# SSD x blocks turned into token rows without TensorE, and gated scores in float32r parts

## The chip, the core and the metric

The kernel runs on one core of a Trainium2 chip. The metric is device time in microseconds of one execution. Five engines work from their own in-order queues: TensorE (PE in the profile; PEld is its weight load), VectorE (DVE), ScalarE (ACT), GpSimd (POOL) and SyncE (SP), which issues nearly all transfers. They meet through semaphores.

## What is computed

The reference is a two-layer trunk over 16 learned tokens and 256 frames, so 272 rows of width 2048. Layer 0 has four gated linear-attention heads (GLA) and eight stick-breaking heads behind one input and one output projection. Layer 1 is an SSD mixer with eight groups of eight heads. Two pieces matter here, cut from it:

```python
# layer 0, a gated head: q_dec = q*exp(g_cum), k_inv = k*exp(-g_cum)
scores = jnp.einsum('bcthk,bcshk->bchts', q_dec, k_inv)
scores = jnp.where(causal, scores, 0.0)
o_intra = jnp.einsum('bchts,bcshv->bcthv', scores, v)

# layer 1, SSD: x after convolution and SiLU, per group
xdt = x * dt[..., None]
cb = jnp.einsum('bctgn,bcsgn->bctsg', c_c, b_c)
y_diag = jnp.einsum('bctsgh,bcsghp->bctghp', l_mat * cb[..., None], xdt)
y = y_diag + y_off + d_skip * x_c
y = _rms_norm_groups(y * jax.nn.silu(z), norm_w, SSM_GROUPS)
```

Everything is float32. The kernel evaluates the scan in a quadratic form over 128 rows.

## The kernel before, in words

**Weights and units.** The work is a list of units of 128 x 2048 weights (1 MB each). An input unit makes 128 output channels for all tokens: 16 blocks of 128 x 128 weights, and for each block three float32r products that stand for one float32 product (L178, L179, L180: high x high, high x low, low x high). An output unit does the same with L494 to L496. So TensorE sees a base stream of products of 272, 260, 256 or 512 columns, 48 to a unit. A unit's weights are loaded by SP into one of three `raw` tiles (L144), and cut into halves; for each half ScalarE writes the high part `whi` (L159) and VectorE, or for some halves GpSimd, the low part `wlo` (L160). There are five buffers of each.

**What sets the order.** Everything else (gates, scans, norms) is written as generators that are stepped once at every quarter unit, a `yield` being one step. What a step issues is placed by a list scheduler that simulates a timeline when the program is built; the order on each engine is then fixed.

**Layer 1.** A group's units come in this order: B, C, four of x, four of z (the gate), and then the four output units of the group two before. `post_x` (L1174) convolves each x unit on ScalarE and VectorE into `xt`, channels on partitions; after every second x unit `x_path` activates two of them. The scan needs x with tokens on partitions, multiplied by dt, in `xd` (128 rows of two blocks) and `xd2` (the last 16 rows). `x_path` gets there by eight TensorE transposes against an identity (L1206) into PSUM, a ninth for the last 16 rows of all four tiles (L1209), and VectorE multiplications out of PSUM (L1218, L1224). `mix_ssd` then multiplies xd with the decay matrices M (L1267) and the last rows (L1273), about six units after the last x unit.

**Layer 0.** The values of both kinds of heads are already turned into token rows in another way: `v_blocks` transposes blocks of 32 x 32 on VectorE (L588, L589), and `to_tokens` writes the result to DRAM (L602, L603) and reads it back with the blocks in their places (L606, L610). In `mix_gla` a gated head's scores are float32 products: L721 (128 x 272, two halves of the contraction), L723 (128 x 144) and L725 (16 x 16).

Of the kernel before, what the change touches and what calls it, by code (L numbers as in the profile page):

```python
# [6 lines left out]
F32 = mybir.dt.float32  # L7
F32R = mybir.dt.float32r
AF = mybir.ActivationFunctionType
ALU = mybir.AluOpType  # L10
PSUM = bass.MemoryType.PSUM

P = 128
# [6 lines left out]
T = NM + S  # L20
# [10 lines left out]
NG, HPG = 8, 8  # L31
# [51 lines left out]
def _wait(*tasks):  # L83
    for t in tasks:
        while not t.done:
            yield


class _Body:
# [621 lines left out]
    def mix_gla(self, h):  # L711
        nc, lp = self.nc, self.lp
        act, vec, mm = nc.scalar.activation, nc.vector, nc.tensor.matmul
        q, k = self.cur["q", h], self.cur["k", h]
        v = self.cur["v", h]
        g = self.cur["r", h]
        yield from _wait(self.tasks["r", h], *[self.tasks["v", h, j] for j in (1, 3)])

        zb = self.zbank()
        for j in range(2):  # L720
            mm(zb[:, 16:288], k[:, j, 0:128], q[:, j, 0:272], start=j == 0, stop=j == 1)  # L721
        for j in range(2):
            mm(zb[:, 288:432], k[:, j, 128:256], q[:, j, 272:416], start=j == 0, stop=j == 1)  # L723
        for j in range(2):
            mm(zb[:16, 0:16], k[:, j, 256:272], q[:, j, 416:432], start=j == 0, stop=j == 1)  # L725
        yield
        s = self.spad
        act(s, zb[:, :432], AF.Copy)
        self.causal(s[:, 16:144], 128, False)
        self.causal(s[:, 288:416], 128, False)  # L730
        self.causal(s[:16, 0:16], 16, False)
        yield
        st = self.s2[h % 2]
        sp = self.parts_of(s, st, (0, 0, 1))[2]
        yield
        u = lp.tile([P, 4, T], F32, tag="gu", name=self.nm("gu"))
        sq = lp.tile([P, T], F32, tag="gsq", name=self.nm("gsq"))
        for j in range(4):
            o = self.po()
            self.values(o, *v, slice(j * P, (j + 1) * P), sp, st)  # L740
            vec.tensor_tensor(u[:, j, :], o[:, :T], g[:, j, :], op=ALU.mult)
            if j == 0:
                act(sq, o[:, :T], AF.Square)
            else:
                s2 = lp.tile([P, T], F32, tag="gs2", name=self.nm("gs2"), bufs=2)
                act(s2, o[:, :T], AF.Square)
                nc.gpsimd.tensor_tensor(sq, sq, s2, op=ALU.add)
            yield
        yield
        qh, ql, _ = self.parts_of(sq)  # L750
        yield
        ms = self.po()
        mm(ms[:, :T], self.ones_r, qh, start=True, stop=False)
        mm(ms[:, :T], self.ones_r, ql, start=False, stop=True)
        yield
        m = lp.tile([P, T], F32, tag="gs2", name=self.nm("gms"), bufs=2)
        r = lp.tile([P, T], F32, tag="grs", name=self.nm("grs"))
        vec.tensor_scalar(m, ms[:, :T], 1.0 / GDV, RMS_EPS, op0=ALU.mult, op1=ALU.add)
        act(r, m, AF.Ln)
        act(r, r, AF.Exp, scale=-0.5)  # L760
        self.newton(r, m, sq)
        yield
        mh, ml = self.mix_tile(h)
        for j in range(4):
            vec.scalar_tensor_tensor(u[:, j, :], u[:, j, :], self.col(C_GN, 4 * h + j), r, op0=ALU.mult, op1=ALU.mult)
            act(mh[:, j, :], u[:, j, :], AF.Copy)
            vec.tensor_tensor(ml[:, j, :], u[:, j, :], mh[:, j, :].bitcast(F32), op=ALU.subtract)
            yield
# [405 lines left out]
    def post_x(self, ps, g, j):  # L1174
# [6 lines left out]
        if j % 2:  # L1181
            self.tasks["x", g, j] = self.push(self.x_path(g, j - 1))

    def x_path(self, g, j):
        nc, vec = self.nc, self.nc.vector
        xt = self.cur["x", g]
        xd = self.cur["xd", g]
        self.silu1(xt[:, j : j + 2, :].rearrange("p a t -> p (a t)"), vec)
        yield
        yield  # L1190
        yield
        if g == 0:
            yield from _wait(self.tasks["dt"])
        if j == 0:
            return
        nc.scalar.activation(self.xq[:, :, :NM], xt[:, :, 256:T], AF.Copy)
        for _ in range(5):
            yield
        pin = self.tc.keep_in_program_order

        pts = [self.po(), self.po()]
        p2 = self.zbank()
        for pt, jj in zip(pts, (0, 2)):
            for i in range(2):
                for t in range(2):
                    pin(nc.tensor.transpose(  # L1206
                        pt[:, t * 256 + i * P : t * 256 + (i + 1) * P], xt[:, jj + i, t * P : (t + 1) * P], self.ident
                    ))
        pin(nc.tensor.transpose(p2[:, :P], self.xq.rearrange("p b t -> p (b t)"), self.ident))  # L1209
        yield  # L1210
        hv = lambda a: a.rearrange("p (h c) -> p h c", c=64)
        bd = lambda a: a.rearrange("p (h o) -> p h o", o=1)
        for pt, jj in zip(pts, (0, 2)):
            h0 = g * HPG + 2 * jj
            c = slice(jj * P, jj * P + 256)
            for t in range(2):
                d = bd(self.est[:, 1, t, h0 : h0 + 4]).broadcast_to([P, 4, 64])
                vec.tensor_tensor(hv(xd[:, t, c]), hv(pt[:, t * 256 : (t + 1) * 256]), d, op=ALU.mult)  # L1218
            yield
        e2 = bd(self.est2[:, 1, g * HPG : (g + 1) * HPG])  # L1220
        for j in range(2):
            for p in range(2):
                h, r = 4 * p + 2 * j, 32 * (2 * p + j)
                vec.tensor_tensor(  # L1224
                    self.xd2[32 * j : 32 * j + 16, 2 * p : 2 * p + 2, :], hv(p2[r : r + 16, :P]),
                    e2[:, h : h + 2, :].broadcast_to([16, 2, 64]), op=ALU.mult,
                )
        yield
# [273 lines left out]
```

## Time and profile before

| | us |
|---|---|
| median of three runs | 1371.52 (1371.16 to 1372.23) |
| the profiled execution | 1372.14 |
| its span | 1370.4 |
| TensorE busy in the span | 1361.3 |
| VectorE busy | 1034.8 |
| ScalarE busy | 790.8 |
| GpSimd busy | 255.3 |

The page gives totals by engine, the chain of work that ended last, and the costliest groups of instructions. A timeline row has start, duration, engine, line, tiles and a count. On TensorE consecutive matmuls overlap in the records, so that a duration there is longer than the distance from one start to the next; the difference of two starts is what the engine needs. A float32 product stands there as two records, a float32r product as one.

### The profile page before, as it was taken

What the parts mean: (1) busy time and instruction counts of PE and PEld (TensorE: products, weight loads), DVE (VectorE), ACT (ScalarE), POOL (GpSimd) and SP (SyncE); (2) the same over time, 40 slices, a digit from 0 to 9 for tenths busy, and PEclk for the clock granted to TensorE, in tenths of its full rate; (3) what the DMA queues carried; (4) which work ended last, traced back from release to release, by engine and by line L of the source; (5) the groups of instructions that cost most, each with busy time, mean ns of one, the idle gap of its engine ahead of it and who ended that gap; (6) DMA issues with size and microseconds to landing.
All of it is one profiled execution on the core that took longest, in us unless ns stands there. A gap on an engine that the chain in (4) does not pass through costs nothing.

```text
span 1370.4 us, 26152 instructions
## 1 busy us (share of the span) xinstructions
PE 1361.3 (99%) x10563; PEld 1313.8 (96%) x10563; DVE 1034.8 (76%) x1747; ACT 790.8 (58%) x1221; POOL 255.3 (19%) x253
## 2 busy tenths in 40 slices
PE   9999999999999999999999999999999999999998
PEld 8999999999999999999999999899898999989986
DVE  7858586685665675568899888787877879877688
ACT  6646455355345554556587888556565655656551
POOL 0000010010001100004400124231422323233221
PEclk9999999999999999999999999999999999999999
DMA  9655546456445455554355665465645565555561
GB/s 328 212 177 193 176 163 210 154 169 208 175 160 183 150 194 175 192 166 158 128 185 176 242 222 210 160 229 185 220 170 208 179 206 213 185 185 185 187 213 62
DMA packets 61945, 256.73 MB, mean 187 GB/s; under 512 B 26176, under 2 KB 29056, under 8 KB 33408
## 3 DMA queue, kind: packets, MB, share of 16 engines
q1 hardware_dynamic: 61104, 254.27, 53.7%
q8 instruction: 83, 1.36, 0.4%
q10 hardware_dynamic: 720, 0.79, 0.2%
q14 instruction: 38, 0.31, 0.1%
HBM read 249.29 MB, written 5.74 MB: 186 GB/s over the span
## 4 chain that ended last, share of the span: by engine, by line
PE 97%; DVE 1%; DMA 1%; ACT 0%; issue 0%; SPq 0%; ACTq 0%
PE pj L178 26%; PE pj L179 26%; PE pj L180 26%; PE pj L494 4%; PE pj L496 4%; PE pj L495 4%; PE po L1267 2%; PE po L633 1%; PE po L1206 1%; DMA raw<-in_wts 0%; PE z L1155 0%; DVE acc L503 0%; DVE fst L1415 0%; PE z L721 0%; DMA hacc<-in_xT 0%; PE z L820 0%
## 5 line engine op out<-in xcount | busy, mean ns | idle before, releaser
L178 PE MATMUL pj<-xhi,whi 128*128 128x272 f32 (+4 forms) x2560 | 732.0, 286 | 1.8 <-ACT xhi L330 0.7
L179 PE MATMUL pj<-xlo,whi 128*128 128x272 f32 (+4 forms) x2560 | 730.2, 286 | 0.0
L180 PE MATMUL pj<-xhi,wlo 128*128 128x272 f32 (+4 forms) x2560 | 729.9, 286 | 0.0
L159 ACT ACTIVATE whi<-raw 128x1024 fp32r<-128x1024 f32 (+2 forms) x434 | 449.2, 1038 | 369.3 <-PE pj L179 296.3
L160 DVE TENSOR_TENSOR wlo<-raw,whi 128x1024 fp32r<-128x1024 f32 (+2 forms) x405 | 504.8, 1251 | 196.5 <-ACT whi L159 192.2
L178 PEld LDWEIGHTS pj<-xhi,whi 128*128 128x128 f32 x2560 | 482.4, 189 | 4.6 <-ACT whi L159 1.7
L179 PEld LDWEIGHTS pj<-xlo,whi 128*128 128x128 f32 x2560 | 482.0, 188 | 1.4 <-issue 0.8
L180 PEld LDWEIGHTS pj<-xhi,wlo 128*128 128x128 f32 x2560 | 481.9, 188 | 0.4 <-issue 0.4
L179 PE MATMUL pj<-mixl,whi 128*128 128x272 f32 x384 | 111.1, 290 | 0.0
L178 PE MATMUL pj<-mixh,whi 128*128 128x272 f32 x384 | 110.7, 289 | 0.1
L180 PE MATMUL pj<-mixh,wlo 128*128 128x272 f32 x384 | 110.2, 287 | 0.0
L160 POOL TENSOR_TENSOR wlo<-raw,whi 128x1024 fp32r<-128x1024 f32 x29 | 74.1, 2557 | 171.8 <-ACT whi L159 157.0
L494 PE MATMUL pj<-whi,yh 128*128 128x512 f32 (+1 forms) x240 | 93.2, 388 | 0.0
L495 PE MATMUL pj<-wlo,yh 128*128 128x512 f32 (+1 forms) x240 | 92.6, 386 | 0.0
L496 PE MATMUL pj<-whi,yl 128*128 128x512 f32 (+1 forms) x240 | 92.2, 386 | 0.0
L179 PEld LDWEIGHTS pj<-mixl,whi 128*128 128x128 f32 x384 | 72.4, 188 | 0.2
L178 PEld LDWEIGHTS pj<-mixh,whi 128*128 128x128 f32 x384 | 72.1, 188 | 0.4 <-ACT mixh L847 0.3
L180 PEld LDWEIGHTS pj<-mixh,wlo 128*128 128x128 f32 x384 | 72.4, 188 | 0.0
L261 POOL TENSOR_TENSOR gr<-gr,gsc 128x1088 f32<-128x1088 f32 x6 | 15.4, 2568 | 287.4 <-ACT gsc L260 287.4
L503 DVE SCALAR_TENSOR_TENSOR acc<-pj,rr,acc 128x512 f32<-128x512 f32 (+1 forms) x65 | 46.5, 733 | 10.9 <-PE pj L496 10.7
L496 PEld LDWEIGHTS pj<-whi,yl 128*128 128x128 f32 x240 | 45.1, 188 | 9.1
L494 PEld LDWEIGHTS pj<-whi,yh 128*128 128x128 f32 x240 | 45.1, 188 | 8.9
(340 smaller groups left out, 1443.6 us busy)
## 6 DMA issues: line engine op xcount, KB each, us to landing
raw<-in_wts SPq DMA_DIRECT2D x212, 1024.0 KB, 4.9
ebc<-edr SPq DMA_DIRECT2D x8, 1664.0 KB, 6.3
raw<-in_wts SPq DMA_DIRECT2D x9, 256.0 KB, 6.4
vdr<-vt SPq DMA_DIRECT2D x8, 256.0 KB, 4.9
vt<-vdr SPq DMA_DIRECT2D x32, 64.0 KB, 2.5
hacc<-in_xT SPq DMA_DIRECT2D x7, 272.0 KB, 5.4
early<-in_wts SPq DMA_DIRECT2D x2, 512.0 KB, 6.8
vdr<-vt SPq DMA_DIRECT2D x8, 128.0 KB, 3.4
```

Of the source, the lines that this page charges most:

```text
L159: self.nc.scalar.activation(hi, src, AF.Copy)
L160: eng.tensor_tensor(lo, src, hi.bitcast(F32), op=ALU.subtract)
L178: mm(ps, whi, xhi, start=first, stop=False)
L179: mm(ps, whi, xlo, start=False, stop=False)
L180: mm(ps, wlo, xhi, start=False, stop=last)
L261: mul(c, c, e, op=ALU.mult)
L494: mm(ps, yh[:, kk, tt], hi[:, k, :], start=kk == 0, stop=False)
L495: mm(ps, yh[:, kk, tt], lo[:, k, :], start=False, stop=False)
L496: mm(ps, yl[:, kk, tt], hi[:, k, :], start=False, stop=kk == 3)
L503: self.nc.vector.scalar_tensor_tensor(a, ps, r[:, t : t + 1], a, op0=ALU.mult, op1=ALU.add)
L633: mm = lambda r, a, b, start=False, stop=False: self.nc.tensor.matmul(r, a, b, start=start, stop=stop, skip_group_check=True)
L1267: pin(mm(ov[p][i * 64 : (i + 1) * 64, jj, t0:S], xd[:, s, h * 64 : (h + 1) * 64], M[:, h, c0:c1], start=(s, jj) == (0, 0), stop=False, **gk,))
```

## The change

The diff has two parts. In `mix_gla` the decayed q and k are cut into a high part (ScalarE) and a low part (VectorE) for the first token block and for the last 16 tokens, and those scores become three float32r products each; the middle product (128 x 144) stays float32. One more step (a quarter unit) lies between the cut and the products. In `x_path` groups 2 to 7 (the third to the eighth) leave for a new generator `x_blocks`, once for every two x units: VectorE transposes 32 x 32 blocks out of `xt` in SBUF, SP writes them to DRAM and reads them back by token rows into the same tile, and six steps later VectorE multiplies them with dt into xd and xd2. Groups 0 and 1 keep the TensorE transposes.

```diff
+        kp = lp.tile([P, 2, 2, 144], F32R, tag="kp", name=self.nm("kp"))
+        qp = lp.tile([P, 2, 2, 288], F32R, tag="qp", name=self.nm("qp"))
+        for p, a, cuts in ((kp, k, ((0, 0, 128), (128, 256, 16))), (qp, q, ((0, 0, 272), (272, 416, 16)))):
+            for o, c, n in cuts:
+                hi = p[:, 0, :, o : o + n]
+                act(hi, a[:, :, c : c + n], AF.Copy)
+                vec.tensor_tensor(p[:, 1, :, o : o + n], a[:, :, c : c + n], hi.bitcast(F32), op=ALU.subtract)
+        abj = [(a, b, j) for a, b in ((0, 0), (0, 1), (1, 0)) for j in range(2)]
+        yield
         zb = self.zbank()
-        for j in range(2):
-            mm(zb[:, 16:288], k[:, j, 0:128], q[:, j, 0:272], start=j == 0, stop=j == 1)
+        for n, (a, b, j) in enumerate(abj):
+            mm(zb[:, 16:288], kp[:, a, j, 0:128], qp[:, b, j, 0:272], start=n == 0, stop=n == 5)
         for j in range(2):
             mm(zb[:, 288:432], k[:, j, 128:256], q[:, j, 272:416], start=j == 0, stop=j == 1)
-        for j in range(2):
-            mm(zb[:16, 0:16], k[:, j, 256:272], q[:, j, 416:432], start=j == 0, stop=j == 1)
+        for n, (a, b, j) in enumerate(abj):
+            mm(zb[:16, 0:16], kp[:, a, j, 128:144], qp[:, b, j, 272:288], start=n == 0, stop=n == 5)
...
+    def x_blocks(self, g, j):
+        nc, vec, sync = self.nc, self.nc.vector, self.nc.sync
+        xt, xd = self.cur["x", g], self.cur["xd", g]
+        vt = self.lp.tile([P, 640], F32, tag="xvt", name=self.nm("xvt"), bufs=2)
+        blk = vt[:, :512]
+        o = blk.rearrange("q (b c x) -> q b c x", c=2, x=32)
+        for i in range(2):
+            vec.transpose(o[:, :, i, :], xt[:, j + i, :256].rearrange("p (b x) -> p b x", x=32))
+            vec.transpose(vt[:, 512 + 32 * i : 544 + 32 * i], xt[:, j + i, 240:T])
+        d = self.tc.dram_tile([4, 32, 8, 64], F32, name=self.nm("xdr"))
+        d9 = self.tc.dram_tile([4, 32, 64], F32, name=self.nm("xdr9"))
+        sync.dma_start(d.rearrange("p t b x -> (p t) (b x)"), blk)
+        sync.dma_start(d9.rearrange("p t x -> (p t) x"), vt[:, 512:576])
+        v = blk.rearrange("q (s p x) -> q s p x", s=2, p=4)
+        for b in range(4):
+            sync.dma_start(v[32 * b : 32 * b + 32], d[:, :, b::4].rearrange("p t s x -> t s p x"))
+        t2 = [vt[32 * i : 32 * i + 16, 512:640] for i in range(2)]
+        for i in range(2):
+            sync.dma_start(t2[i].rearrange("q (p x) -> q p x", p=4), d9[:, 16:, 32 * i : 32 * i + 32].rearrange("p t x -> t p x"))
+        for _ in range(6):
+            yield
...
         self.silu1(xt[:, j : j + 2, :].rearrange("p a t -> p (a t)"), vec)
         yield
+        if g > 1:
+            yield from self.x_blocks(g, j)
+            return
```

TensorE in group 3, in the third z unit (`pj` is the unit's PSUM tile, `xhi` and `xlo` the parts of the layer's input). Before:

```order
L179 MATMUL pj_11509<-xlo,whi_11450 128x256
L180 MATMUL pj_11509<-xhi,wlo_11451 128x256
L1206 MATMUL po_11526<-ident,xt_11148 128x128 x4
L1206 MATMUL po_11527<-ident,xt_11148 128x128 x4
L1209 MATMUL z_64<-ident,xq 128x128
L178 MATMUL pj_11509<-xhi,whi_11450 128x256
L179 MATMUL pj_11509<-xlo,whi_11450 128x256
```

Of the change, the same place:

```order
L178 MATMUL pj_11642<-xhi,whi_11579 128x256
L179 MATMUL pj_11642<-xlo,whi_11579 128x256
L180 MATMUL pj_11642<-xhi,wlo_11580 128x256
L178 MATMUL pj_11642<-xhi,whi_11579 128x256
L179 MATMUL pj_11642<-xlo,whi_11579 128x256
```

The nine transposes are gone and nothing took their place; in layer 1 all else on TensorE stands where it stood.

VectorE in group 3, from the second pair of x tiles to the first output unit. Before:

```order
L1089 TENSOR_TENSOR xt_11148<-xt_11148,xcl_11398 128x544
L160 TENSOR_TENSOR wlo_11558<-raw_11447,whi_11557 128x1024
L160 TENSOR_TENSOR wlo_11596<-raw_11507,whi_11595 128x1024
L1085 TENSOR_SCALAR xcl_11537<-gz_11445 128x512
L1218 TENSOR_TENSOR xd_11149<-po_11526,est 128x256 x2
L1218 TENSOR_TENSOR xd_11149<-po_11527,est 128x256 x2
L1224 TENSOR_TENSOR xd_8248<-z_64,est_8840 16x128 x4
L160 TENSOR_TENSOR wlo_11624<-raw_11507,whi_11623 128x1024
L160 TENSOR_TENSOR wlo_11657<-raw_11592,whi_11656 128x1024
L160 TENSOR_TENSOR wlo_11704<-raw_11652,whi_11703 128x1024
```

Of the change (`xvt` is the tile of blocks, `est` holds dt):

```order
L1098 TENSOR_TENSOR xt_11242<-xt_11242,xcl_11513 128x544
L1201 STREAM_TRANSPOSE xvt_11531<-xt_11242 128x8x32
L1202 STREAM_TRANSPOSE xvt_11531<-xt_11242 128x32
...
L160 TENSOR_TENSOR wlo_11712<-raw_11640,whi_11711 128x1024
L1219 TENSOR_TENSOR xd_11243<-xvt_11370,est 128x128 x4
L1228 TENSOR_TENSOR xd_8320<-xvt_11370,est_8912 16x128 x2
L1094 TENSOR_SCALAR xcl_11661<-gz_11574 128x512
L160 TENSOR_TENSOR wlo_11740<-raw_11640,whi_11739 128x1024
L160 TENSOR_TENSOR wlo_11773<-raw_11708,whi_11772 128x1024
L1219 TENSOR_TENSOR xd_11243<-xvt_11531,est 128x128 x4
L1228 TENSOR_TENSOR xd_8320<-xvt_11531,est_8912 16x128 x2
L160 TENSOR_TENSOR wlo_11820<-raw_11768,whi_11819 128x1024
```

The multiplications of a pair moved away from its transposes: three weight splits stand between those of the second pair, which was one stretch before.

SP in the same stretch of the change; before, only the weight loads stand there:

```order
L144 DMA raw_11640<-in_wts 128x2048
L1205 DMA xdr_11375<-xvt_11370 128x512
L1206 DMA xdr_1368_11376<-xvt_11370 128x64
L144 DMA raw_11708<-in_wts 128x2048
L1209 DMA xvt_11370<-xdr_11375 32x8x64 x4
L1212 DMA xvt_11370<-xdr_1368_11376 16x4x32 x2
L144 DMA raw_11768<-in_wts 128x2048
L1205 DMA xdr_11536<-xvt_11531 128x512
L1206 DMA xdr_1384_11537<-xvt_11531 128x64
L1209 DMA xvt_11531<-xdr_11536 32x8x64 x4
L1212 DMA xvt_11531<-xdr_1384_11537 16x4x32 x2
L144 DMA raw_11815<-in_wts 128x2048
```

Sixteen transfers a group came in between the loads; the first pair's write has one load between it and its reads, the second pair's none.

More of the change, by code (lines that the diff above doesn't have):

```diff
@@ L1182, in post_x @@
             self.tasks["x", g, j] = self.push(self.x_path(g, j - 1))
+    def x_blocks(self, g, j):
[19 more added lines that the diff above has]
+            yield
+        h0 = g * HPG + 2 * j
+        for s in range(2):
+            for c in range(2):
+                e = self.est[:, 1, s, h0 + 2 * c : h0 + 2 * c + 2].rearrange("q (h p x) -> q h p x", p=1, x=1)
+                vec.tensor_tensor(
+                    xd[:, s, (j + c) * P : (j + c + 1) * P].rearrange("q (h p x) -> q h p x", p=2, x=32),
+                    v[:, s].rearrange("q (h p) (c x) -> q h p c x", p=2, c=2)[:, :, :, c, :],
+                    e.broadcast_to([P, 2, 2, 32]), op=ALU.mult,
+                )
+        yield
+        e2 = self.est2[:, 1, g * HPG : (g + 1) * HPG].rearrange("p (h o) -> p h o", o=1)
+        for i in range(2):
+            h = 2 * (j + i)
+            vec.tensor_tensor(
+                self.xd2[32 * i : 32 * i + 16, j : j + 2, :], t2[i].rearrange("p (h c) -> p h c", c=64),
+                e2[:, h : h + 2, :].broadcast_to([16, 2, 64]), op=ALU.mult,
+            )
+        yield
     def x_path(self, g, j):
```

## The prediction

> **What bounds the kernel now.** I read the page's totals and chain first, then its costliest groups, the waits, and the busy times of one steady stretch.
>
> ```profile
> span 1370.4 us, 26152 instructions
> PE 1361.3 (99%) x10563; PEld 1313.8 (96%) x10563; DVE 1034.8 (76%) x1747; ACT 790.8 (58%) x1221; POOL 255.3 (19%) x253
> PE 97%; DVE 1%; DMA 1%; ACT 0%; issue 0%; SPq 0%; ACTq 0%
> L178 PE MATMUL pj<-xhi,whi 128*128 128x272 f32 (+4 forms) x2560 | 732.0, 286 | 1.8 <-ACT xhi L330 0.7
> L160 DVE TENSOR_TENSOR wlo<-raw,whi 128x1024 fp32r<-128x1024 f32 (+2 forms) x405 | 504.8, 1251 | 196.5 <-ACT whi L159 192.2
> ```
> ```profile
> ACT whi L159 <- PE pj L179: 296.3, 226, 2.2
> SPq L144 <- DVE wlo L160: 617.0, 142, 11.0
> ```
> ```profile
> 935.00:1020.00 85.00, 85.00 (x642) 80.30 (x641) 65.80 (x103) 50.27 (x71) 24.31 (x18) 1.00 0.54 191
> ```
>
> TensorE is busy from end to end: 97% of the chain is its own, and the largest group of products idles 1.8 us in 732. The second fence says who waits for whom. ScalarE makes the high parts of the weights as soon as TensorE frees one of five buffers (226 waits on TensorE), and the load queue waits for VectorE to free a raw buffer (617 us), not VectorE for loads. So the supply runs ahead of TensorE by its buffers. The last fence is one steady group of the SSD layer (columns: TensorE, weight loads, VectorE, ScalarE, GpSimd busy, granted clock, DMA share): TensorE 85.00 of 85 us, VectorE 65.80, DMA 54%, clock 1.00. Here a TensorE instruction that goes away shortens the span by its own pitch, start to start, and work added to the others costs nothing while it stays inside their slack. A matmul's listed 286 ns is latency; the pitch has to be read from starts.
>
> **Transposes removed (groups 3 to 8, numbered 2 to 7 in the code).** TensorE in group 3 of the code:
>
> ```profile
> 942.12 0.28 PE L180 MATMUL pj<-xhi,wlo 128*128 128x256 f32 x1
> 942.24 1.04 PE L1206 MATMUL po<-ident,xt 128*128 128x128 f32 x8
> 943.12 0.27 PE L1209 MATMUL z<-ident,xq 128*128 128x128 f32 x1
> ...
> 943.46 0.28 PE L180 MATMUL pj<-xhi,wlo 128*128 128x256 f32 x1
> ```
>
> From L180 to L180 is 1.34 us. It holds three ordinary products (L180, then L178 and L179 in the gap), 0.113 each as the stretch ahead of it runs, so 0.34; the nine transposes cost 1.00 us. Six groups do the same nine: **-6.0 us**.
>
> **The pitch of the gate products after them.** The same z units, 8 us before and 8 us behind those transposes, and 6 us behind the transposes of groups 2 and 6:
>
> ```profile
> 932.00:940.00 8.00, 8.00 (x73) 8.00 (x73) 6.54 (x8) 5.41 (x8) 2.40 (x1) 1.00 0.56 204
> 944.60:952.60 8.00, 8.00 (x70) 8.00 (x69) 3.84 (x8) 4.30 (x6) 2.95 (x2) 1.00 0.43 163
> 862.00:868.00 6.00, 6.00 (x55) 6.00 (x55) 4.00 (x8) 3.29 (x5) 2.67 (x2) 1.00 0.52 180
> 1200.00:1206.00 6.00, 6.00 (x53) 6.00 (x52) 2.02 (x2) 2.41 (x4) 2.84 (x2) 1.00 0.48 175
> ```
>
> 73 products against 70, and 55 against 53, at the same clock: about 4%, or 4.5 ns each, and it lasts until other work comes between. By starts the step up lies behind the transposes in groups 3, 5 and 6 (some 250 products); in group 2 the slow stretch lies ahead of them (some 100), and they ended it: there some 85 fast ones may turn slow. Net (250 - 85) x 4.5 ns = **-0.7 us**. The bounds: all 6 x 192 products fast, 350 x 4.5 ns = -1.6; all slow, 800 x 4.5 ns = +3.6. I take the near value because what stands ahead of the z units does not change.
>
> **Scores.** One head of the gated layer now, two pieces:
>
> ```profile
> 83.93 0.29 PE L180 MATMUL pj<-xhi,wlo 128*128 128x272 f32 x1
> 84.06 0.62 PE L721 MATMUL z<-gq,gk 128*128 128x272 f32 x2
> ...
> 84.77 0.29 PE L180 MATMUL pj<-xhi,wlo 128*128 128x272 f32 x1
> ...
> 85.64 0.28 PE L178 MATMUL pj<-xhi,whi 128*128 128x272 f32 x1
> 85.76 0.62 PE L721 MATMUL z<-gq,gk 128*128 128x272 f32 x2
> 86.22 0.65 PE L723 MATMUL z<-gq,gk 128*128 128x144 f32 x4
> 86.80 0.27 PE L725 MATMUL z<-gq,gk 128*16 128x16 f32 x4
> ...
> 87.35 0.29 PE L178 MATMUL pj<-xhi,whi 128*128 128x272 f32 x1
> ```
> ```profile
> 427.12 0.42 PE L799 MATMUL z<-qe,ke 128*128 128x272 f32 x2
> 427.37 0.28 PE L179 MATMUL pj<-xlo,whi 128*128 128x272 f32 x1
> ...
> 428.48 0.29 PE L179 MATMUL pj<-xlo,whi 128*128 128x272 f32 x1
> ...
> 428.73 0.45 PE L801 MATMUL z<-qe,ke 128*128 128x144 f32 x3
> 429.02 0.22 PE L803 MATMUL z<-qe,ke 128*16 128x16 f32 x3
> ...
> 429.44 0.28 PE L179 MATMUL pj<-xlo,whi 128*128 128x272 f32 x1
> ```
>
> One float32 product of 272 columns (two records): 0.84 less three ordinary ones of 0.1235 is 0.47. The second fence shows the same shape in float32r in the stick-breaking heads: two in 0.25, so six cost 0.75 in place of 2 x 0.47 = 0.94: 0.19 gained per head. Small products: the second piece is 1.71 - 0.37 = 1.34; without its large product 0.87 remain for two of 144 columns, which stay, and two of 16. Four records of 16 columns start in 0.20 (86.80 to the next, 87.00), at most 0.29 with a share of the rest. Six in float32r: of 0.96 - 0.37 = 0.59 in the second fence, 0.125 and 0.29 belong to the larger shapes, so three cost 0.17 and six at most 0.35, at least 0.25 by halves of what is drain. That is a loss of 0 to 0.15. Per head 0.04 to 0.19; I take 0.12, four heads: **-0.5 us**.
>
> **What is added, and what hides it.** Per group VectorE gets four large and four small block transposes and eight multiplications of 128x128 in place of four of 128x256; the four of 16 rows stay four. The block transposes and the read-back exist in the gated layer:
>
> ```profile
> L588 DVE STREAM_TRANSPOSE vt<-pj 128x256 f32<-128x256 f32 x24 | 10.3, 439 | 12.1 <-PE pj L180 12.0
> L589 DVE STREAM_TRANSPOSE vt<-pj 128x32 f32<-128x32 f32 x24 | 3.9, 171 | 0.0
> L1218 DVE TENSOR_TENSOR xd<-po,est 128x256 f32<-128x256 f32 x32 | 11.7, 412 | 1.6 <-PE po L1206 1.6
> L624 DVE TENSOR_TENSOR gvl<-vt,gvh 128x128 fp32r<-128x128 f32 x16 | 4.0, 291 | 0.9 <-ACT gvh L623 0.7
> ```
> ```profile
> vdr<-vt SPq DMA_DIRECT2D x8, 256.0 KB, 4.9
> vt<-vdr SPq DMA_DIRECT2D x32, 64.0 KB, 2.5
> ```
> ```profile
> L606 SPq DMA_DIRECT2D vt<-vdr x64: 557/608/1407, 34.2 to 623.9; - x64
> ```
> ```profile
> 938.98 0.73 DVE L1089 TENSOR_TENSOR xt<-xt,xcl 128x544 f32<-128x544 f32 x1 [1.14 <-ACT xcl L1088]
> 954.30 1.23 DVE L160 TENSOR_TENSOR wlo<-raw,whi 128x1024 fp32r<-128x1024 f32 x1 [4.38 <-ACT whi L159]
> ```
> ```profile
> 960.06 1.73 PE L1267 MATMUL po<-M,xd 128*64 128x256 f32 x14
> ```
>
> VectorE per group: 4 x 0.44 + 4 x 0.17 + 8 x 0.29 - 4 x 0.41 = +3.1 us on 65.8 of 85, so it still idles 15. Its splits of k and q in layer 0 (estimate from the multiplications above, 800 columns and two small ones: 1.5 us a head) lie in a layer that is looser. ScalarE's half of those splits is as long, and it works 58% of the span.
>
> The one thing that can reach TensorE is the age of xd. The later pair of x tiles in group 3: activated at 939.7; transposes, with the first pair's in the way, to 942.2; write 0.3 + 4.9 us to 947.4; four reads and two small ones issue in 6 x 0.6 = 3.6, the last lands 2.5 later, 953.5; six multiplications of at most 0.29, 955.2. Its reader, the scan's products (L1267), starts at 960.06, a microsecond sooner after the change: 3.9 us of margin. On the SP queue the reads stand ahead of a weight load and wait there 5 us for the write; behind them the load is late by as much, and its raw tile has a buffer of lead. On VectorE the multiplications wait some 3 us, with splits queued behind them, in the 4.38 us that it now idles there. Taken at nothing. If that cover were gone, twelve waits of 3 us would be 36 us.
>
> Sum: -6.0 - 0.7 - 0.5 = -7.2 us. The profiled execution took 1372.14 around its span of 1370.4, 0.6 above the median of 1371.52; the shift applies to either, so the median becomes **1364.3 us**.
>
> **Rivals.** (a) The read-back is late (slower). The four strided reads cost more here, beside the broadcast loads of the decays, and the scan's products wait in each of six groups. The point is 3.9 us of lateness for any wait at all and 3.9 + 7.2/6 = 5.1 for the whole gain; at 6 us late the sum is 1364.3 + 6 x 2.1 = 1377. For it: everything hangs on one in-order queue. Against it: 64 KB landed in 2.5 us in layer 0 under the same load. In the Trainium skill, VectorE: DVE Perf Modes (The three transpose paths) warns that a plain strided copy for a transpose is far slower than the transposing DMA, and its rules for authors send a 128x128 transpose to TensorE; by that rule this rival would be the likeliest, and the 2.5 us row disagrees, as the pieces read here are contiguous runs.
> (b) All z products fall into the slow pitch: 1364.3 + 0.7 + 3.6 = 1368.6. For it: the pitch does step; against it: five of six groups enter z in the fast one.
> (c) The weight supply sets the time, and TensorE waits for what it gained: 1371.5, no change. For it: 99% busy may hide a match of rates; against it: the load queue waits for buffers, 617 us of it.
>
> **How the numbers follow.** Forecast 0.84, (a) 0.04, (b) 0.08, (c) 0.04. A measurement tells about 0.2%, 2.7 us, from no change, so faster means under 1368.8: the forecast and half of (b), 0.88; within: the rest of (b) and (c), 0.08; slower: 0.04. The range, 1362.2 to 1368.0, takes the sum from -9.3 (all z fast, the best score case, 0.15 us a group more for the transposes) up to most of (b).
>
> **What would show it.** Right: no identity transposes of x left in groups 2 to 7, steady groups about 1.1 us shorter, TensorE's busy share still 99%, waits of the xd multiplications on the read-back but none of the scan's products. Wrong: idle time of TensorE ahead of the scan's products or of weight products behind a late split, a slower pitch in z, or landings of the read-back well over 2.5 us.

## The result and the profile after

The changed kernel takes 1364.49 us (median of six runs, 1363.65 to 1366.38) against 1371.87 us (1371.16 to 1372.40) for the kernel before, run beside it: a ratio of 0.9952, with a 95% interval of 0.9943 to 0.9962. The forecast was 1364.3 us. As the experiments below show, that agreement is partly luck: one term of the sum was too small, and a cost that the sum put at nothing was there.

The totals and the chain of the page of the changed kernel (its profiled execution took 1365.87 us):

```profile
span 1363.8 us, 26308 instructions
PE 1353.3 (99%) x10525; PEld 1307.0 (96%) x10525; DVE 1056.2 (77%) x1835; ACT 794.1 (58%) x1231; POOL 257.5 (19%) x253
PE 90%; DVE 5%; DMA 2%; issue 1%; SPq 1%; ACT 0%; ACTq 0%; DVEq 0%
L494 PE MATMUL pj<-whi,yh 128*128 128x512 f32 (+1 forms) x240 | 93.5, 389 | 2.3 <-DVE acc L503 2.3
xvt<-xdr SPq DMA_DIRECT2D x48, 64.0 KB, 2.5
```

TensorE has 38 records fewer and 8.0 us less busy time, but the span fell by only 6.6. TensorE's share of the chain went from 97% to 90%, VectorE's from 1% to 5% and the transfers' from 1% to 2%: somewhere TensorE now waits. Where, the windows of three groups show (columns as in the prediction):

```profile
927.00:1010.00 83.00, 83.00 (x627) 78.34 (x626) 66.02 (x115) 49.93 (x70) 24.61 (x18) 1.00 0.63 220
1010.50:1093.50 83.00, 83.00 (x627) 78.34 (x626) 70.36 (x118) 49.75 (x70) 23.43 (x18) 1.00 0.59 205
1094.00:1177.00 83.00, 80.94 (x609) 75.94 (x608) 70.44 (x114) 48.69 (x69) 22.35 (x18) 1.00 0.59 205
```

The first two are full; the third, group 5, lacks 2.06 us of TensorE. The starts of the scan's products say the same. They are listed here for groups 3 to 6:

```profile
955.97 0.65 PE L1320 MATMUL po<-M,xd 128*64 128x256 f32 x4
1039.21 0.65 PE L1320 MATMUL po<-M,xd 128*64 128x256 f32 x4
1122.45 0.65 PE L1320 MATMUL po<-M,xd 128*64 128x256 f32 x4
1208.02 0.65 PE L1320 MATMUL po<-M,xd 128*64 128x256 f32 x4
```

From one group to the next it is 83.24 and 83.24 us, where the same starts of the kernel before were 84.3 to 84.7 apart, and then 85.57. The place itself, on TensorE, VectorE and GpSimd:

```profile
1134.94 0.39 PE L496 MATMUL pj<-whi,yl 128*128 128x512 f32 x1
1137.38 0.47 PE L494 MATMUL pj<-whi,yh 128*128 128x512 f32 x1 [2.06 <-DVE acc L503]
```
```profile
1105.00 0.72 DVE L1098 TENSOR_TENSOR xt<-xt,xcl 128x544 f32<-128x544 f32 x1
1108.73 3.03 DVE L1219 TENSOR_TENSOR xd<-xvt,est 128x128 f32<-128x128 f32 x4 [3.00 <-DMA xvt<-xdr]
...
1112.30 0.45 DVE L1201 STREAM_TRANSPOSE xvt<-xt 128x256 f32<-128x256 f32 x1
...
1128.46 0.81 DVE L1145 TENSOR_SCALAR M<-ebc,est 128x256 f32<-128x256 f32 x3
...
1129.98 6.60 DVE L1145 TENSOR_SCALAR M<-ebc,est 128x144 f32<-128x144 f32 x13
1136.49 1.40 DVE L503 SCALAR_TENSOR_TENSOR acc<-pj,rr,acc 128x512 f32<-128x512 f32 x2
```
```profile
1108.61 2.39 POOL L160 TENSOR_TENSOR wlo<-raw,whi 128x1024 fp32r<-128x1024 f32 x1 [13.24 <-ACT whi L159]
...
1131.20 2.46 POOL L160 TENSOR_TENSOR wlo<-raw,whi 128x1024 fp32r<-128x1024 f32 x1
```

TensorE waits for L503, VectorE's addition of a finished output unit to `acc`, which frees the PSUM tile that TensorE wants. That addition stands behind the decay factors of the next group (L1145), and these take 6.60 us for 13 where group 3 takes 4.44. The reason for the 6.60 is in the GpSimd rows: one factor that starts beside GpSimd's split of 1131.20 lasts until that split is over. The kernel before had the same 6.59 us in this place and was early enough to bear it:

```profile
1131.89 0.82 DVE L1136 TENSOR_SCALAR M<-ebc,est 128x256 f32<-128x256 f32 x3 [1.50 <-PE po L1267]
...
1133.41 6.59 DVE L1136 TENSOR_SCALAR M<-ebc,est 128x144 f32<-128x144 f32 x13
1139.93 1.40 DVE L503 SCALAR_TENSOR_TENSOR acc<-pj,rr,acc 128x512 f32<-128x512 f32 x2
```

There VectorE idled 1.50 us for the scan's products before it began. In the changed kernel it begins 2.95 us after TensorE has gone on to the next output unit (1125.51). It is late because at 1108.73 it first waited 3.00 us for the read-back, then lost 2.1 us to the split that GpSimd had begun 0.12 us earlier, and only then came to the second pair's block transposes, which could have run at 1105.7. So the theory after the result was: the 2.06 us (and 0.28 us in group 2, the other group where a GpSimd split falls beside the factors) are a **stall** made by two things together, VectorE's lateness and GpSimd's splits, and not the price of the transfers as such.

### The profile page after: what moved, and what is told of

It is laid out like the page before. It is cut to its first block, busy times and chain, and to the rows that moved or that the text cites. A ratio compares the mean times of both kernels' runs of the same rounds, so it can differ in the third digit from the quotient of the medians.

```text
span 1363.8 us, 26308 instructions
## 1 busy us (share of the span) xinstructions
PE 1353.3 (99%) x10525; PEld 1307.0 (96%) x10525; DVE 1056.2 (77%) x1835; ACT 794.1 (58%) x1231; POOL 257.5 (19%) x253
## 4 chain that ended last, share of the span: by engine, by line
PE 90%; DVE 5%; DMA 2%; issue 1%; SPq 1%; ACT 0%; ACTq 0%; DVEq 0%
PE pj L178 25%; PE pj L179 25%; PE pj L180 25%; PE pj L494 3%; PE pj L495 3%; PE pj L496 3%; DMA xdr<-xvt 1%; PE po L1320 1%; PE po L633 1%; DVE M L1145 1%; DVE wlo L160 1%; DMA xvt<-xdr 1%; SPq L1209 1%; DVE acc L503 1%; PE z L1164 0%
## 5 line engine op out<-in xcount | busy, mean ns | idle before, releaser
L495 PEld LDWEIGHTS pj<-wlo,yh 128*128 128x128 f32 x240 | 45.1, 188 | 8.7
```

Source lines behind the costliest of these rows:

```text
L495: mm(ps, yh[:, kk, tt], lo[:, k, :], start=False, stop=False)
```

## Experiments: the stall

Three variants ran beside the changed kernel itself (`again`). The rival was that the added transfers or the weight supply make the scatter and the lost 2 us (supply).

**`again`: no edit.**

> The changed kernel once more, beside the three variants. Theory (stall): in its profile VectorE comes 2.95 us late to the decay factors M of group 5, because the first x pair's multiplications wait 3.00 us for their read-back and then 2.1 us for a split on GpSimd, ahead of the second pair's transposes; while it makes M, one of these lasts 2.43 us beside another GpSimd split; TensorE then stands 2.06 us for the sums of the output projection (0.29 us in group 2). Six runs of it spread over 2.7 us (1363.65 to 1366.38), the kernel before over 1.2 us: the theory reads that spread as this stall, there in full in some runs and absent in the fastest. So: median 1364 to 1366, spread 2 us or more. Rival (supply): the spread comes from the added transfers or the weight loads; then the variants below spread as much.

Measured: 1364.27 us (1363.37 to 1366.31), 0.9953 of the kernel before (0.9940 to 0.9967); a spread of 2.9 us. Its profiled execution happened to be one without a stall, span 1361.7 us, 2.1 below the first one. The same place on VectorE, and the GpSimd split:

```profile
1107.36 0.90 DVE L1219 TENSOR_TENSOR xd<-xvt,est 128x128 f32<-128x128 f32 x4 [1.48 <-DMA xvt<-xdr]
...
1108.80 0.45 DVE L1201 STREAM_TRANSPOSE xvt<-xt 128x256 f32<-128x256 f32 x1
```
```profile
1108.77 2.40 POOL L160 TENSOR_TENSOR wlo<-raw,whi 128x1024 fp32r<-128x1024 f32 x1 [13.24 <-DVE xd L1228]
```

Here the read-back landed 1.37 us sooner, ahead of the split; the four multiplications took 0.90 us in place of 3.03, and the transposes started 3.5 us sooner. It is one program: which of the two comes first differs from one execution to another.

**`behind`: in group 5 the first pair's multiplications stand behind the second pair's transposes.**

```diff
-        for _ in range(6):
+        for _ in range(10):
             yield
+        last = [i for i in self.traced() if i.engine == mybir.EngineType.DVE][-1]
...
+                self.tc.add_manual_dep(one.ins, last.name, free, reason="late")
```

Each of the six multiplications (`one`) is ordered behind `last`, the last VectorE instruction recorded by then. On VectorE this changes the order in group 5 alone.

> One thing is moved: in group 5 the six multiplications of the first x pair stand behind the second pair's block transposes on VectorE, as they do in the other groups by chance or not at all. Stall theory: the second pair's transposes start near 1106 instead of 1112.3, its read-back lands about 6 us sooner, M begins at most 1.2 us behind the scan's products, the stall of 2.06 us falls to 0.3 or less; the profiled span falls to about 1361.8, the median to 1363.6 or below, the spread to about 1.2 us. Supply rival: no change of median or spread, a gap of 1 to 2 us elsewhere.

Measured: 1364.43 us (1363.02 to 1364.78), 0.9949 (0.9937 to 0.9962). The spread fell to 1.8 us, the stall to 0.91, the median not at all:

```profile
1136.15 0.47 PE L494 MATMUL pj<-whi,yh 128*128 128x512 f32 x1 [0.91 <-DVE acc L503]
```

The transposes did start at 1105.66, but their write landed so that the reads were issued at 1111.77, and the multiplications still met the split (2.81 us for four). M began 1.2 us sooner than in the first profile, not 1.8 as expected. This edit is half a remedy, and its expectation was too bold.

**`nosplit`: two of GpSimd's splits go to VectorE.**

```diff
-            pool = h == 1 and n >= 24 and n % 3 == 0
+            pool = h == 1 and n >= 24 and n % 3 == 0 and n % 42 != 33
```

> The two splits that GpSimd does while VectorE makes the decay factors of groups 2 and 5 go to VectorE. Stall theory: no M factor lasts 2.4 us, M takes 4.4 us in every group instead of 6.6 in two, both gaps go (VectorE may be up to 3.0 us late before TensorE waits, and is 2.95 late in group 5), against 1.25 us more VectorE work right behind: span about 1361.7, median about 1363.6, spread 1.2 us. If the length of M has no part in it (only the late read-back), the gap of 2 us stays.

Measured: 1364.24 us (1363.48 to 1364.62), 0.9949 (0.9937 to 0.9962); spread 1.1 us.

```profile
1129.67 4.43 DVE L1145 TENSOR_SCALAR M<-ebc,est 128x144 f32<-128x144 f32 x13
1134.03 1.22 DVE L160 TENSOR_TENSOR wlo<-raw,whi 128x1024 fp32r<-128x1024 f32 x1
1135.16 1.40 DVE L503 SCALAR_TENSOR_TENSOR acc<-pj,rr,acc 128x512 f32<-128x512 f32 x2
```
```profile
1136.05 0.47 PE L494 MATMUL pj<-whi,yh 128*128 128x512 f32 x1 [0.83 <-DVE acc L503]
```

The 13 factors are back to 4.43 us, as the theory said; but the split that VectorE now does itself stands just ahead of the addition, and 0.83 us of the stall is left. The median, expected at 1363.6, did not fall either. A gap of 0.91 or 0.83 us in one profile each does not by itself refute the supply rival, since the unedited kernel shows 2.06 us in one profile and none in the next; what does stands at the end of this section.

**`both`: the two edits together.**

> Both edits at once. Stall theory: no gap over 0.2 us in the groups, the least lateness of VectorE, span about 1361.5, median 1363.4, 0.5 to 1.5 us under the changed kernel, spread 1.2 us or less. Were the two effects independent costs of TensorE time, they would add up to more than either alone; by the theory they do not add, since both take away the same gap.

Measured: 1363.33 us (1363.13 to 1363.95), 0.9943 (0.9931 to 0.9956), spread 0.8 us, no gap in the groups:

```profile
span 1361.2 us, 26305 instructions
PE 97%; DVE 2%; issue 0%; ACT 0%; ACTq 0%; DVEq 0%
```

The chain is TensorE's own again. The two effects do not add up, they take away one gap, as the theory wanted. This is called the stall-free variant below.

**`again2` and `both2`: the changed kernel and that variant side by side on another chip.**

> The changed kernel a third time, on another chip, beside the stall-free variant. Stall theory: 0.9945 to 0.9955 of the kernel before and a spread of 2 us or more, as the stall in group 5 comes and goes with the order in which the read-back lands and GpSimd's split starts.

> The stall-free variant a second time, on the same chip as the run above. Stall theory: 0.6 to 1.2 us under the changed kernel's median, ratio 0.9940 to 0.9946, spread about 1 us; its fastest run no more than 0.4 us under the changed kernel's fastest, since a run without the stall should take the same. If the difference of the first comparison was chance, the medians agree within 0.3 us.

Measured: 1364.79 us (1364.18 to 1367.68), 0.9955 (0.9941 to 0.9968), against 1363.09 us (1362.87 to 1363.73), 0.9941 (0.9928 to 0.9953). The medians are 1.7 us apart here and 0.9 us in the first comparison, and in both comparisons the variant's median lies under the changed kernel's fastest run. The ratios' intervals overlap, so the size of the difference stays rough. The profile of `again2` has the stall again, 1.98 us, after a wait of 4.39 us for the read-back. Two points were missed: the medians lie further apart than the 0.6 to 1.2 us expected, and the fastest runs are 1.3 us apart, not 0.4. That no run of the changed kernel was free of the stall on that chip would explain both, but only one of its five runs has a profile, so it is not shown. The variant is the fastest kernel of this study.

The profiles also settle what TensorE waits for. In group 5, count from the start of the output unit that follows the scan's products (1125.51 in the first profile) to the start of the first addition behind the factors (1136.49 there), and set TensorE's wait beside it:

| profile | addition starts after, us | TensorE waits, us |
|---|---|---|
| changed kernel, first | 10.98 | 2.06 |
| `again2` | 10.90 | 1.98 |
| `behind` | 9.84 | 0.91 |
| `nosplit` | 9.76 | 0.83 |
| `both` | 8.81 | none |
| `again` | 8.28 | none |
| `both2` | 7.35 | none |

Wherever there is a wait, it is the first number less 8.92 or 8.93 us: the wait is what this addition is late by. In none of these profiles does TensorE wait for weights in the groups; its waits there of more than 0.1 us are all for L503. That refutes the supply rival as it stood. The added transfers have a part in the stall, but by way of VectorE, whose lateness begins with the landing of the read-back.

## Experiments: the terms of the sum

**`scores`: the gated scores alone, on the kernel before.** The edit is the first part of the change, without the second.

> The kernel before with the gated heads' scores in float32r parts alone. The prediction's term: 0.12 us per head, -0.5 us in all (bounds -0.16 to -0.76). Read from the changed kernel's trace: a head's two pieces cost 0.50 and 0.98 us beyond the ordinary products, 1.48, against 0.47 + 1.34 = 1.81 before, so -0.33 per head and -1.3 us in all; then the small products of 16 columns were mis-sized, not the large one. If the splits of q and k on VectorE and ScalarE cost TensorE time, less than -0.5 or slower.

Measured: 1369.84 us (1369.29 to 1370.45) against 1371.43, 0.9988 (0.9979 to 0.9997): -1.6 us. One head on TensorE:

```profile
86.51 0.28 PE L178 MATMUL pj<-xhi,whi 128*128 128x272 f32 x1
86.63 0.66 PE L730 MATMUL z<-qp,kp 128*128 128x272 f32 x4
87.12 0.29 PE L179 MATMUL pj<-xlo,whi 128*128 128x272 f32 x1
...
88.12 0.41 PE L730 MATMUL z<-qp,kp 128*128 128x272 f32 x2
88.36 0.65 PE L732 MATMUL z<-gq,gk 128*128 128x144 f32 x4
88.76 0.40 PE L734 MATMUL z<-qp,kp 128*16 128x16 f32 x6
89.01 0.37 PE L178 MATMUL pj<-xhi,whi 128*128 128x272 f32 x1
```

The six large products take 0.49 + 0.24 = 0.73 us, as costed (0.75). The small ones were costed wrongly. Middle and small products together took 0.78 us before (86.22 to 87.00 in the prediction's fence) and take 0.65 now (88.36 to 89.01), though the four middle records are unchanged and the small ones became six: 0.13 gained where a loss of 0 to 0.15 was costed. The change-over is where it went: from the first middle record to the first small one it was 0.58 us and is 0.40. Counted as the prediction did, beyond the ordinary products between them, a head's two pieces fell from 1.81 to 1.48, 1.3 us for four heads; the interval of the ratio holds that as well as the 1.6.

**`xclean`: the x part alone, with the stall removed.**

> The x part alone, with the two edits of the run before it that take the stall away (first pair's multiplications behind the transposes in group 5, two splits from GpSimd to VectorE); the scores are as before. The prediction's terms: -6.0 for 54 transposes and -0.7 for the pitch of the gate products, -6.7 us. With both parts the stall-free kernel took 7.9 us off, so -6.5 if the scores are worth 1.3, and -7.3 if they are worth 0.5. If the added transfers cost TensorE anything, less.

Measured: 1365.12 us (1364.78 to 1366.27) against 1371.43, 0.9953 (0.9940 to 0.9965): -6.3 us. The forecast's terms were -6.7; in the profiles of this run and of the kernel before, groups 2 to 7 alone are 6.8 us shorter by starts. With the scores' -1.6 the two parts make -7.9, and `both` measured -7.9 and -8.5: they add up.

**`dead`: the stall-free variant with the nine identity transposes back in each of the six groups, their results unread.**

```diff
+                            self.tc.keep_in_program_order(nc.tensor.transpose(
+                                pt[:, t * 256 + i * P : t * 256 + (i + 1) * P], xt[:, jj + i, t * P : (t + 1) * P], self.ident
+                            ))
...
+                    self.tc.keep_in_program_order(nc.tensor.transpose(p2[:, :P], xt[:, 3, P : 2 * P], self.ident))
```

> The stall-free variant with both parts, and in groups 2 to 7 the nine identity transposes put back on TensorE at their old distance, their results read by nobody (the output is the reference's all the same). By the prediction: +6.0 us over the stall-free variant (54 at 0.111), and the slow pitch of the gate products is back behind the transposes in some groups: +0.7, at most +3.6 (a step from 113.5 to 118 ns in the starts of some 150 to 800 products). If the transposes were partly hidden behind weight loads, under +5. If the pitch does not depend on them, +6.0 with 113.5 ns throughout.

Measured: 1370.28 us (1369.69 to 1370.95), 0.9991 (0.9982 to 1.0000), 6.7 to 7.4 us over the stall-free variant by the medians of its two series (each taken against the kernel before beside it). That is the transposes' 6.0 and the pitch: six microseconds of gate products ahead of and behind the transposes of group 3, in `dead`, and in `both`, where none stand:

```profile
934.00:940.00 6.00, 6.00 (x55) 6.00 (x54) 4.47 (x8) 4.81 (x8) 0.24 (x1) 1.00 0.93 243
944.00:950.00 6.00, 6.00 (x53) 6.00 (x52) 1.63 (x3) 3.50 (x5) 1.95 (x2) 1.00 0.27 66
```
```profile
941.00:947.00 6.00, 6.00 (x55) 6.00 (x54) 3.21 (x5) 4.72 (x7) 1.55 (x1) 1.00 0.41 137
```

53 against 55, as in the kernel before. By starts, the 118 ns are back behind the transposes of groups 3, 5 and 6 and of no other, and in group 2 the transposes end them. The pitch hangs on the transposes.

**`late`: the blocks are copied once more in DRAM, so that the read-back comes later.**

```diff
+        dd = self.tc.dram_tile([4, 32, 8, 64], F32, name=self.nm("xdrb"))
+        sync.dma_start(dd.rearrange("p t b x -> (p t) (b x)"), d.rearrange("p t b x -> (p t) (b x)"))
+        d = dd
```

> The stall-free variant with the blocks copied once more from DRAM to DRAM before they are read back (256 KB, like the write, which landed in 3.8 us), so that each read-back comes some 4 to 5 us later. The order of the program is laid anew by estimated ready times, so the multiplications and in places the scan's products stand further back. Rival (a) of the prediction: past 3.9 us of lateness the scan's products wait; at 5 us 1.1 us in each of six groups, +6.6 us; and VectorE, waiting 3 us more at twelve places with splits queued behind, may add some. If the order makes room for it, no change within 1 us: then it is the order laid with the transfers' times in mind that hides the read-back, and not the 3.9 us.

Measured: 1370.93 us (1367.00 to 1374.54), 0.9992 (0.9982 to 1.0002), 7.4 to 8.0 us over the stall-free variant by medians, in 7.5 us of scatter. The copy landed in 3.1 us, and the scan's products now wait. Waits of the page, and group 3:

```profile
DVE xd L1234 <- DMA xvt<-xdr: 27.1, 11, 6.4
PE po L1327 <- DVE xd L1224: 4.5, 4, 1.7
```
```profile
956.22 1.08 PE L1327 MATMUL po<-M,xd 128*64 128x256 f32 x8
958.99 0.65 PE L1327 MATMUL po<-M,xd 128*64 128x256 f32 x4 [1.68 <-DVE xd L1224]
960.18 2.45 PE L1327 MATMUL po<-M,xd 128*64 128x256 f32 x20 [0.54 <-DVE xd L1224]
```

In group 3 they pause 1.68 and 0.54 us, and VectorE waits up to 6.4 us at one place. The mechanism of rival (a) is thus real: with one copy more in the chain nearly the whole gain is gone, although the order was laid anew around the later data. Its price is not confirmed. The scan's products wait in three groups of the six (3, 5 and 7), 4.5 us in all, and in group 3 more was lost than the waits. Behind the two pauses the granted clock (the last column but two) fell to a half:

```profile
961.00:964.00 3.00, 3.00 (x25) 2.73 (x22) 3.00 (x4) 0.00 (x0) 0.00 (x0) 0.50 0.47 104
```

There pairs of products of 144 columns start 0.24 us apart, where in `both` it is 0.12. At a half for some 3.4 us that is an estimated 1.7 us; what makes up the rest of the loss stays open. The single pause of 2.06 us in the changed kernel left the clock at 1.00.

Why rival (a) did not happen in the changed kernel is only in part the margin of the prediction. In group 3 it was there. In group 4 the second pair's multiplications ended behind the start of the scan's products (1039.21):

```profile
1038.12 2.50 DVE L1219 TENSOR_TENSOR xd<-xvt,est 128x128 f32<-128x128 f32 x4 [3.02 <-DMA xvt<-xdr]
```

TensorE did not wait, because the scan takes the first pair's heads first; by the starts of the single products the closest of these multiplications was done some 0.3 us before the product that reads it. Group 7 had some 1.2 us.

**`group1`: the stall-free variant with group 1 converted as well (`if g > 1` becomes `if g > 0`).**

> The stall-free variant with group 1 also going through the block transposes (nine identity transposes fewer, seven groups in place of six). By the prediction's price: -1.0 us more, 1362.4 or 0.9936 of the kernel before. The condition is the margin of group 1, where no output projection stands between its x tiles and the scan's products, and the order of the scan's products is laid anew, further back: if its read-back is late there, the scan's products wait and the gain is gone.

Measured: 1364.04 us (1362.96 to 1364.76), 0.9946 (0.9934 to 0.9958): no gain over the stall-free variant, where 1362.4 was expected. Nine transposes fewer, but the scan's products of group 1 wait 0.66 us for the late rows of xd, and other small gaps of 0.15 and 0.58 us appear later:

```profile
825.47 0.26 PE L1330 MATMUL po<-mt,xd 128*64 128x32 f32 x4
826.38 0.31 PE L1330 MATMUL po<-mt,xd 128*64 128x32 f32 x4 [0.66 <-DVE xd L1231]
```

**`flip`: one unread identity transpose in group 2, behind the first gate tile.**

> The stall-free variant with one identity transpose more, read by nobody, in group 2 behind the first gate tile, between the second and the third product of a weight tile. In group 2 alone the gate products run at the slow pitch to the end (118 ns, some 165 of them) in the changed kernel, and the transposes put back ended that. If any product put in between can turn the pitch: 113.5 ns from there on, some 140 products at 4.5 ns less 0.11 for the transpose, -0.5 us, in the starts if not in the median. If the pitch depends on what and where it is: still 118 ns behind it, +0.1 us.

Measured: 1363.67 us (1363.04 to 1364.34), 0.9943 (0.9927 to 0.9958). The transpose ran in the third gate unit, at 860.10, and the 47 gate products behind it (140 were expected) still start 118 ns apart. One product in between did not turn the pitch here. In `group1`, where the order ahead of them was laid anew, the gate products of group 2 start some 113.5 ns apart to the end. What sets the pitch stays open.

## Why the prediction was right, and where it was not

- **The bound.** Right: TensorE was the bound, and what it no longer does comes off the span. Steady groups are 83.24 us long, 1.1 to 1.4 less; TensorE is busy 99%.
- **Transposes, -6.0.** Right. Both with the pitch's 0.7 in them, `dead` gives 6.7 to 7.4 and `xclean` 6.3.
- **Pitch, -0.7.** Right in sign, place and size: by starts the products at 118 ns fell from some 330 to 165, 165 x 4.5 ns = 0.7. All that was foreseen for group 2 came too: its slow stretch now runs to the end.
- **Scores, -0.5.** The mechanism was right, the size not: 1.3 us by starts, 1.6 by the times, outside the bounds of 0.04 to 0.19 per head. The step that failed is the residue of 0.87 us, which was shared out between the middle and the small product as if neither changed the other. It holds a change-over from the middle to the float32 small product that goes away with the latter.
- **"Taken at nothing."** Half right. The scan's products never waited, and in group 3 their margin was about what the chain gave: the multiplications ended at 951.2 and the scan began at 955.97. But that margin was taken for all six groups, and in group 4 only some 0.3 us were left: that it held there was luck. And the age of xd was not "the one thing that can reach TensorE": a late VectorE reached it through the addition that frees its PSUM tile. VectorE's waits were set against "the 4.38 us that it now idles there", an idle stretch of group 3, and the cover was taken to be the same in six groups. Groups are not alike: of every third unit the second half is split on GpSimd, a group has 14 units, and so groups 2 and 5 have a split beside the decay factors. The row of 6.59 us in group 5 was in the trace before. The cost is 2.3 us in a run with the stall and nothing in one without, 0.9 to 1.7 us in the medians.
- **The sum.** -6.0 - 0.7 - 1.3 = -8.0, the stall-free variant's -7.9 and -8.5; the changed kernel's three medians -6.8 to -7.4. A term too small by 0.8 and a cost left out met at 1364.3.
- **Rivals.** (a) did not happen; `late` shows that it can, at a price that does not follow its sum. The rule of the Trainium skill that stood beside it (VectorE: DVE Perf Modes, Rules for kernel authors: a 128 x 128 transpose belongs to TensorE) would have left 6 to 7 us on TensorE here; `dead` is that kernel's TensorE, and the trace disagrees with the rule where TensorE is the bound. (b) and (c) are refuted by the starts and by the full windows.

## What to carry to other kernels

Where one engine is busy from end to end, count its instructions in starts and move them to engines with slack; that part of the forecast (-6.7 us) came out to some tenths of a microsecond. The slack of the other engines is not a sum over the span but the lateness at one place: take it in the group where it is least, and look for the work that falls differently from group to group. A multiplication that used to read PSUM and now reads only SBUF has become one that GpSimd can hold up.

## What the runs showed of the hardware

**VectorE waits for GpSimd when both work in SBUF.** The lines of the factors and of the new multiplications in the changed kernel, and the old multiplication of the kernel before (shortest, median and longest in ns):

```profile
L1145 DVE TENSOR_SCALAR M<-ebc,est x80: 280/342/2432, 876.4 to 1216.7; 128x256 f32<-128x256 f32 x40, 128x144 f32<-128x144 f32 x40
...
L1219 DVE TENSOR_TENSOR xd<-xvt,est x48: 268/284/2424, 859.8 to 1291.3; 128x128 f32<-128x128 f32 x48
```
```profile
L1218 DVE TENSOR_TENSOR xd<-po,est x32: 401/412/425, 752.7 to 1283.5; 128x256 f32<-128x256 f32 x32
```

The one that reads PSUM never varied by more than 24 ns, though only two of the 32 began while GpSimd was at work. Of the 16-row multiplications out of PSUM of the kernel before (L1224) nine did, and all 32 lasted 269 to 294 ns. Of the 72 new ones (48 of 128 rows and 24 of 16) seven lasted 0.8 to 2.4 us; each had begun while GpSimd was at work, and each ended some 0.15 us after GpSimd's instruction did. So the 3.1 us of VectorE time that the prediction added per group came with a dependence that the old instructions did not have. The Trainium skill says so in SBUF — State Buffer (SBUF: two separate sides): an exclusive lock for a whole instruction, which a VectorE operation with two SBUF inputs takes too when the GpSimd one reads SBUF. The trace agrees, with 2.42 us for an instruction of 0.28.

**The landing of the same reads varies by 3 us from run to run.** The first pair's read-back of group 5 released VectorE at 1107.36, 1108.73 and 1110.26 in three profiles of the same program, whose reads were issued within 0.9 us of each other. A margin under 3 us at such a place is there in some runs only, and the spread of the times (2.7 to 3.5 us in three series of the changed kernel, 0.8 and 0.9 in the two of the stall-free variant) is how it is seen from outside.
